# Norm weights spread by TensorE, places for all of o's split weights, v copied by ScalarE, and the query/key convolutions inside the heads' side chains

## The chip, the cores and the metric

The kernel runs on one core of a Trainium2 chip. The metric is the device time of one execution in microseconds (us). Engines are named as in the profile: PE is the matrix engine (PEld its weight loads), DVE the vector engine, ACT the scalar engine with the activation functions, POOL the general engine, SP the engine that issues the DMAs.

## The reference

One layer of a hybrid decoder trunk, T = 1024 tokens and D = 1024 channels, all in float32:

```
h = rms_norm(x, norm_pre_w)
proj = h @ w_in                       # columns for s5, pool, sconv, mlstm (qk, v, o, i, f), z paths, gates
qk = silu(causal_depthwise_conv(qk, conv_w))      # 4 taps, q and k, 4 heads of 128
y_d = mlstm(q, k, v, sigmoid(o), i, f)            # chunks of 64, exponential gates
y_a = s5_ssm(...); y_b = pool_mixer(...); y_c = short gated convolution
branches = y * silu(z)
merged = sum_b sigmoid(gate_b) * (branch_b @ w_branch[b])
out = x + rms_norm(merged @ w_out, norm_post_w)
```

## The kernel before

Each float32 matmul operand is split into a high and a low part (ACT copies the high part, DVE or POOL subtracts it from the operand for the low part), and a product takes three matmuls: high by high, high by low, low by high. One matmul of 128x512 is called a *mm* here.

The front of the program: `phase0` loads x in 8 tiles of 128 tokens. `norm(t)` squares a tile on ACT, works out the root on DVE with tiny operations, and multiplies by root and norm weights (`wpre`, the 4 KB row spread over 128 partitions by a 512 KB DMA) on DVE, at L332; `turn(t)` transposes the tile on PE (`tp`, L341) and splits it into `bh` (ACT, L344) and `bl` (DVE, L345). For the first two tiles the orders of SP, ACT, DVE and POOL are those of the program text; then a scheduler orders every engine from the text's priorities, and pools with a fixed count of places add waits. `load_vectors` fetches small vectors (`vrows`), `if_weights` the 8 columns of the mLSTM's input and forget gates (`ifraw`, 1,024 rows of 32 bytes) and splits them into two tiles `wif`. v's projection takes 24 mm for each of 8 tiles (L364), whose sum is copied from PSUM as `vst` and stored. `if_proj` takes 32 mm with `wif`; its sums `ifp` are copied by ACT to `ifsb` (L447), turned on PE (`iftp`, L455) and made into the gates by a chain of small DVE and ACT operations that ends in `lf` and a matmul `bps` (L480). o's projection has the same form as v's, with 8 weight tiles split into `o2h` (ACT) and `o2l` (POOL). `combos` forms sums of the operand's quarters (`t1f`, `t2f`, `t3f`, on DVE and POOL, L376, and split into `bht` and `blt`), with which the further products are made by Strassen's scheme, seven products of 12 mm for four quarters.

Then four heads: `qk_pair(h)` makes one such set of seven products (84 mm) for q and k into four tiles `xc`, and runs the 4-tap convolution on each: ACT scales the first tap into `cacc` (L561), DVE adds three taps (L563), ACT takes the sigmoid (L565), POOL multiplies (L566). `mlstm_head(h)` is a *side chain*: a generator that emits one step each time the main text ticks it, once after each product. Beside the chain, the main text emits the S5 inputs (heads 0 and 1) and gate products (heads 2 and 3). A product's two groups of 12 mm may share one PSUM bank, whose first contents are moved by an ACT copy `p<-p` (L213) before the second group may begin. Afterwards comes the S5 stage (`s5_gen`, a long DVE chain that first delivers `wr` to the PE transposes `wps`), beside more gate products, and then the gated paths, merges and the output.

The places for split weights, and the wait that the head's chain has before its first scores:

```
CFG = {"wr": 4, "w": 8, "ws": 3, "u": 3, "g": 12, "m": 4, "mm": 5, "sd": 3, "g2": 17}
def alloc(n):
    if len(self.wo) < 4:
        return self.wp.tile([P, HALF], F32R, tag="w", name=self.nm(n))
    return self.slot(n, dt=F32R)          # a place of "g"
...
prep(0)
for _ in range(ML_TICKS):                 # 3
    yield
scores(0)
```

Of the kernel before, what the change touches and what calls it, by code (L numbers as in the profile page):

```python
# [31 lines left out]
EARLY = ((0,), (1,), (2,), (3, 4))  # L32
ORDER = (3, 0, 1, 2)
PACE = 2
ML_TICKS = 3
DMA_SCRATCH = 1024
CFG = {"wr": 4, "w": 8, "ws": 3, "u": 3, "g": 12, "m": 4, "mm": 5, "sd": 3, "g2": 17}
MAGIC = 12582912.0
# [10 lines left out]
class Kern:  # L49
# [48 lines left out]
            return self.g2.tile(list(shape), dt, tag="g2", name=self.nm(name))  # L98
        return self.gp.tile(list(shape), dt, tag="g", name=self.nm(name))

    def stage(self, name, shape=(P, HALF)):
        return self.gp.tile(list(shape), F32, tag="m", name=self.nm(name))

    def u(self, name, shape=(P, HALF)):
        return self.wp.tile(list(shape), F32, tag="u", name=self.nm(name))
# [141 lines left out]
    def phase0(self):  # L247
        nc, io = self.nc, self.io
        x, wpre = io["x"], io["norm_pre_w"]
        names = ("11", "12", "21", "22")  # L250
        self.B = {n: (self.blk([P, 4, HALF], F32R, "bh" + n), self.blk([P, 4, HALF], F32R, "bl" + n)) for n in names}
        self.wv, self.wo = [], []
        wb = self.blk([P, D], F32, "wpre")
        self.warm_up()
        xs = {}

        def load(t, parts):
            xs[t] = self.blk([P, 2, D], F32, "x")
            n = D // parts
            for i in range(parts):  # L260
                nc.sync.dma_start(out=xs[t][:, 0, i * n:(i + 1) * n], in_=x[0, t * P:(t + 1) * P, i * n:(i + 1) * n])

        E = mybir.EngineType
        with self.tc.manual_schedule(engines={E.SP, E.Activation, E.DVE, E.Pool}):
            load(0, 2)
            nc.sync.dma_start(out=wb, in_=wpre.partition_broadcast(P))
            raw = [self.wp.tile([P, HALF], F32, tag="wr" if k < 4 else "ws", name=self.nm("raw")) if k < 7 else self.stage("raw")
                   for k in range(8)]
            hl = []
            for k in range(8):  # L270
                two = k < 6
                hl.append((self.slot("o2h", dt=F32R, two=two), self.slot("o2l", dt=F32R, two=two)))
            self.wv = hl

            def fetch(k):
                nc.sync.dma_start(out=raw[k], in_=io["w_in"][0, k * P:(k + 1) * P, C_V:C_V + HALF])

            def hi(k):
                nc.scalar.activation(out=hl[k][0], in_=raw[k], func=AF.Copy)

# [12 lines left out]
            lo(1, ve)  # L293
            self.turn(0, xs[0])
            hi(3)
            lo(2, po)
            lo(3, ve)
            self.norm(1, xs[1], wb)
            for k in range(4, 8):
                hi(k)  # L300
                lo(k, po if k % 2 == 0 else ve)
            self.turn(1, xs[1])
        for t in range(2, 8):
            load(t, 1)
            self.norm(t, xs[t], wb)
            self.turn(t, xs[t])
# [114 lines left out]

    def if_weights(self):
        nc = self.nc
        raw = self.u("ifraw", (P, 8, 8))
        nc.sync.dma_start(out=raw, in_=self.io["w_in"][0, :, C_IF:C_IF + 8].rearrange("(k p) c -> p k c", p=P))
        self.wif = []
        for kk in range(2):
            w = self.wp.tile([P, 4, P], F32R, tag="w", name=f"wif{kk}")
            r = raw[:, kk * 4:kk * 4 + 4, :]
            nc.gpsimd.memset(w.bitcast(F32), 0.0)  # L430
            nc.vector.tensor_copy(out=w[:, :, 0:8], in_=r)
            nc.vector.tensor_tensor(out=w[:, :, 8:16], in0=r, in1=w[:, :, 0:8].bitcast(F32), op=ALU.subtract)
            self.wif.append(w)

    def if_proj(self):
        nc = self.nc
        self.ifsb = []
        for hf in range(2):
            ps = self.bank("ifp")
            n = 0  # L440
            for i in range(2):
                for k in range(8):
                    nc.tensor.matmul(out=ps, lhsT=self.wif[k // 4][:, k % 4, :], rhs=self.B[f"{k // 4 + 1}{hf + 1}"][i][:, k % 4, :],
                                     start=(n == 0), stop=(n == 15))
                    n += 1
            sb = self.u("ifsb", (16, HALF))
            nc.scalar.activation(out=sb, in_=ps[0:16, :], func=AF.Copy)  # L447
            self.ifsb.append(sb)
# [93 lines left out]
    def qk_pair(self, h):  # L542

        nc = self.nc
        xc = {(i, hf): None for i in range(2) for hf in range(2)}

        def dest(i, hf):
            xc[i, hf] = self.slot("xc", (P, HALF + 3), two=True)
            return xc[i, hf][:, 3:HALF + 3], lambda t: t
        self.strassen(C_QK + h * P, C_QK + W + h * P, dest)  # L550
        out = []
        for i in range(2):
            ct = i * 4 + h
            w = lambda k: self.vec[:, k * 8 + ct:k * 8 + ct + 1]
            nc.gpsimd.memset(xc[i, 0][:, 0:3], 0.0)
            nc.vector.tensor_copy(out=xc[i, 1][:, 0:3], in_=xc[i, 0][:, HALF:HALF + 3])
            res = []
            for hf in range(2):
                x = xc[i, hf]
                acc = self.slot("cacc", two=True)  # L560
                nc.scalar.activation(out=acc, in_=x[:, 0:HALF], func=AF.Copy, scale=w(0))  # L561
                for k in range(1, 4):
                    nc.vector.scalar_tensor_tensor(out=acc, in0=x[:, k:k + HALF], scalar=w(k), in1=acc, op0=ALU.mult, op1=ALU.add)  # L563
                sg = x[:, 0:HALF]
                nc.scalar.activation(out=sg, in_=acc, func=AF.Sigmoid)  # L565
                nc.gpsimd.tensor_tensor(out=acc, in0=acc, in1=sg, op=ALU.mult)  # L566
                res.append(acc)
            out.append(res)
        return out

    def mlstm_head(self, h, qT, kT):

        nc = self.nc
        sc = float(P) ** -0.5
        cols = slice(h * P, (h + 1) * P)
        st = {}

        def prep(hf):
            hs_ = slice(hf * HALF, (hf + 1) * HALF)
# [88 lines left out]
            nc.sync.dma_start(out=self.yscr[3][cols, d["hs_"]], in_=y)  # L668

        prep(0)  # L670
        for _ in range(ML_TICKS):
            yield
        scores(0)
        prep(1)
        yield
        states(0)
        yield
        outputs(0, 0)
# [621 lines left out]
    def run(self):  # L1300
        nc, tc = self.nc, self.tc
        self.setup()
        with tc.tile_pool(name="g2a", bufs=CFG["g2"]) as self.g2:
            self.phase0()
            self.load_vectors()
            rc = self.const.tile([P, 16], F32, name="rcnt")
            rci = self.const.tile([P, 16], I32, name="rcnti")
            nc.gpsimd.iota(rci, pattern=[[1, 16]], base=1, channel_multiplier=0)
            nc.vector.tensor_copy(out=rc, in_=rci)
            nc.vector.reciprocal(out=rc, in_=rc)  # L1310
            self.rcnt = rc
            self.if_weights()
            for t in range(8):
                ps = self.proj_o2(self.wv, t)
                st = self.u("vst")
                nc.vector.tensor_copy(out=st, in_=ps)
                nc.sync.dma_start(out=self.vscr[t * P:(t + 1) * P, :], in_=st)
            self.if_proj()

# [15 lines left out]
            self.combos_last(full)
            between = (lambda: self.s5_u(0), lambda: self.s5_u(2), lambda: None, lambda: None)
            for h in range(4):
                qT, kT = self.qk_pair(h)
                self.sides.append(self.mlstm_head(h, qT, kT))
                between[h]()  # L1340
                for n in EARLY[h]:
                    self.keep_gates(*GATES[n])
            self.drain()
# [82 lines left out]
```

## Time and profile before

| | |
|---|---|
| device time, median of 3 runs | 1312.68 us (1310.72 to 1317.19) |
| profiled execution, device time | 1319.64 us |
| its span | 1317.9 us |
| PE busy in the span | 1250.6 us (95%) |
| DVE, POOL, ACT busy | 887.5, 714.5, 508.6 us |
| granted PE clock, mean | 0.972 of full speed |

The profile is one execution; every time below is on its clock, which starts with the span. It lies 7 us above the median of the runs. In a timeline row the two numbers are start and duration, and the brackets hold the idle time of the engine just before, with what ended it.

### The profile page before, as it was taken

Reading aid. Unit: us, or ns where it says so; the run is one execution under the profiler, and the core shown is the slowest. Engines: PE = TensorE matmul, PEld = TensorE weight load, DVE = VectorE, ACT = ScalarE, POOL = GpSimd, SP = SyncE. Lnnn points to the kernel's source line nnn. Section 1 sums busy time; section 2 is a strip of 40 time slices with the busy share of each in tenths; the row PEclk is TensorE's granted clock in tenths of the full one; section 3 lists DMA queues with packets and bytes.
Section 4 is the critical chain, followed back from the end, with each engine's and each line's share of the span. In section 5 each row is a group of like instructions: output and inputs, shape, how many; then the busy total and the mean of one; then the engine's idle time right before and its main releaser. Section 6 shows DMA issues by size and latency. Waiting matters only on the chain.

```text
span 1317.9 us, 17475 instructions
## 1 busy us (share of the span) xinstructions
PE 1250.6 (95%) x5790; PEld 1009.6 (77%) x5790; DVE 887.5 (67%) x1481; ACT 508.6 (39%) x930; POOL 714.5 (54%) x568
## 2 busy tenths in 40 slices
PE   7989999999989989999999989999999989979997
PEld 5867778787778757677778867888788868858886
DVE  7693886868774988689966776576856375443433
ACT  6223536365555433323344734233322232333221
POOL 4271675857555546455545454555575656678340
PEclk8989999999989989899999999999999999979999
DMA  7301333434435334443544666345554565597441
GB/s 237 109 25 64 98 111 114 113 112 108 124 102 140 93 84 112 105 116 93 142 114 137 167 193 217 98 154 155 182 171 150 161 191 155 185 370 248 126 154 48
DMA packets 211210, 183.76 MB, mean 139 GB/s; under 512 B 35916, under 2 KB 155296, under 8 KB 211120
## 3 DMA queue, kind: packets, MB, share of 16 engines
q1 hardware_dynamic: 211120, 182.65, 46.3%
q8 instruction: 46, 0.75, 0.2%
q14 instruction: 44, 0.36, 0.1%
HBM read 125.94 MB, written 54.56 MB: 137 GB/s over the span
## 4 chain that ended last, share of the span: by engine, by line
PE 58%; DVE 10%; DMA 6%; issue 3%; POOL 3%; ACT 1%; SPq 0%; DVEq 0%; POOLq 0%; ACTq 0%
PE p L155 35%; PE br L155 11%; PE out L155 7%; DMA raw<-in_w_in_dram 3%; DVE s L207 2%; POOL wlo L134 2%; DMA y<-yscr 1%; PE glu L155 1%; DMA raw<-in_w_branch_dram 1%; PE yps L1098 1%; PE yps L1097 1%; PE xps L1063 0%; PE yps L1100 0%; DVE Z L1080 0%; DMA m<-mscr 0%
## 5 line engine op out<-in xcount | busy, mean ns | idle before, releaser
L134 POOL TENSOR_TENSOR wlo<-raw,whi 128x512 fp32r<-128x512 f32 x166 | 234.1, 1412 | 223.2 <-ACT whi L130 146.2
L134 POOL TENSOR_TENSOR wlo<-s,whi 128x512 fp32r<-128x512 f32 x152 | 219.5, 1445 | 146.9 <-ACT whi L130 72.1
L155 PE MATMUL p<-bht,whi 128*128 128x512 f32 x608 | 170.3, 397 | 3.5 <-DVE u L201 1.6
L155 PE MATMUL p<-blt,whi 128*128 128x512 f32 x608 | 167.1, 394 | 0.0
L155 PE MATMUL p<-bht,wlo 128*128 128x512 f32 x608 | 166.2, 393 | 0.0
L130 ACT ACTIVATE whi<-raw 128x512 fp32r<-128x512 f32 x166 | 102.5, 618 | 156.7 <-PE p L155 94.2
L155 PE MATMUL p<-bh,whi 128*128 128x512 f32 x456 | 128.9, 403 | 17.0 <-ACT p L213 5.5
L130 ACT ACTIVATE whi<-s 128x512 fp32r<-128x512 f32 x152 | 95.0, 626 | 126.2 <-PE p L155 104.0
L207 DVE TENSOR_TENSOR s<-raw,raw 128x512 f32<-128x512 f32 x76 | 69.4, 913 | 99.2 <-DMA raw<-in_w_in_dram 84.2
L155 PEld LDWEIGHTS p<-bht,whi 128*128 128x128 f32 x608 | 113.2, 189 | 29.2 <-issue 4.4
L155 PEld LDWEIGHTS p<-blt,whi 128*128 128x128 f32 x608 | 114.5, 190 | 23.9 <-issue 0.2
L155 PEld LDWEIGHTS p<-bht,wlo 128*128 128x128 f32 x608 | 113.7, 189 | 23.6 <-issue 0.2
L155 PE MATMUL p<-bl,whi 128*128 128x512 f32 x456 | 128.3, 401 | 0.0
L155 PE MATMUL p<-bh,wlo 128*128 128x512 f32 x456 | 124.2, 393 | 0.5 <-POOL wlo L134 0.5
L155 PEld LDWEIGHTS p<-bh,whi 128*128 128x128 f32 x456 | 85.2, 191 | 38.3 <-ACT p L213 6.8
L155 PEld LDWEIGHTS p<-bl,whi 128*128 128x128 f32 x456 | 87.7, 194 | 18.7
L155 PEld LDWEIGHTS p<-bh,wlo 128*128 128x128 f32 x456 | 86.6, 191 | 19.7 <-POOL wlo L134 1.4
L155 PE MATMUL br<-yzh,whi 128*128 128x512 f32 x256 | 74.0, 405 | 12.0 <-ACT yzh L130 11.4
L155 PE MATMUL br<-yzl,whi 128*128 128x512 f32 x256 | 69.7, 392 | 0.0
L155 PE MATMUL br<-yzh,wlo 128*128 128x512 f32 x256 | 68.5, 389 | 0.0
L155 PEld LDWEIGHTS br<-yzh,whi 128*128 128x128 f32 x256 | 49.7, 195 | 24.6 <-ACT yzh L130 13.3
L1204 DVE TENSOR_TENSOR sg<-br,sg 128x512 f32<-128x512 f32 x64 | 43.6, 686 | 36.1 <-PE br L155 23.3
(433 smaller groups left out, 2222.3 us busy)
## 6 DMA issues: line engine op xcount, KB each, us to landing
raw<-in_w_in_dram SPq DMA_DIRECT2D x168, 256.0 KB
gscr<-sg SPq DMA_DIRECT2D x64, 256.0 KB
sg<-gscr SPq DMA_DIRECT2D x64, 256.0 KB
y<-yscr SPq DMA_DIRECT2D x48, 256.0 KB
mscr<-sg SPq DMA_DIRECT2D x48, 256.0 KB
m<-mscr SPq DMA_DIRECT2D x48, 256.0 KB
raw<-in_w_branch_dram SPq DMA_DIRECT2D x40, 256.0 KB
x<-in_x_dram SPq DMA_DIRECT2D x18, 256.0 KB
```

Source lines behind the costliest of these rows:

```text
L130: nc.scalar.activation(out=hi, in_=src, func=AF.Copy)
L134: eng.tensor_tensor(out=lo, in0=src, in1=hi.bitcast(F32), op=ALU.subtract)
L155: self.nc.tensor.matmul(out=out, lhsT=a(k), rhs=b(k), start=(n == 0 and not more), stop=(n == last), skip_group_check=more)
L207: tt(out=t, in0=a, in1=b, op=op)
L1097: nc.tensor.matmul(out=yps[gp][:, jj, :], lhsT=Tt[:, gl, :], rhs=V[:, gl, :], start=True, stop=False)
L1098: nc.tensor.matmul(out=yps[gp][:, jj, :], lhsT=car[q, jj, 0:8, :].rearrange("q d p -> q (d p)"), rhs=X[q, 0, jj, :], start=False, stop=False)
L1204: nc.vector.tensor_tensor(out=sg, in0=bps, in1=sg, op=ALU.mult)
```

## The change

It has four parts. The row of norm weights is loaded as 4 KB, before x, and spread by two matmuls of a column of ones with it, each 512 columns wide, whose results DVE copies into `wpre`. The gate columns go into one constant tile `wif` of 240 columns, of which overlapping slices of 128 columns are the weights; the split parts of v's last two weight tiles go to the places of "m", and one raw tile to a place of "u", so that the 8 places of "w" and the 12 of "g" hold nothing when o's weights come. v's copy out of PSUM goes from DVE to ACT. The convolution leaves `qk_pair` and becomes part of the head's side chain, with a yield after each DVE step of a pair of tiles; the chain has 14 steps where it had 11.

```diff
-ML_TICKS = 3
+            nc.sync.dma_start(out=wrow, in_=wpre)
             load(0, 2)
-            nc.sync.dma_start(out=wb, in_=wpre.partition_broadcast(P))
+            for i in range(2):
+                ps = self.bank("wps")
+                nc.tensor.matmul(out=ps, lhsT=ones, rhs=wrow[:, i * HALF:(i + 1) * HALF], start=True, stop=True)
+                nc.vector.tensor_copy(out=wb[:, i * HALF:(i + 1) * HALF], in_=ps)
...
-                two = k < 6
-                hl.append((self.slot("o2h", dt=F32R, two=two), self.slot("o2l", dt=F32R, two=two)))
+                alloc = (lambda n: self.slot(n, dt=F32R, two=True)) if k < 6 else (lambda n: self.stage(n, dt=F32R))
+                hl.append((alloc("o2h"), alloc("o2l")))
...
-        for kk in range(2):
-            w = self.wp.tile([P, 4, P], F32R, tag="w", name=f"wif{kk}")
...
+        self.wif = self.const.tile([P, 8 * 16 + 112], F32R, name="wif")
+        nc.gpsimd.memset(self.wif.bitcast(F32), 0.0)
+        w = self.wif[:, 0:P].rearrange("p (k c) -> p k c", c=16)
+        nc.vector.tensor_copy(out=w[:, :, 0:8], in_=raw)
+        nc.vector.tensor_tensor(out=w[:, :, 8:16], in0=raw, in1=w[:, :, 0:8].bitcast(F32), op=ALU.subtract)
...
+    def qk_conv(self, h, xc, out, i, hf):
+        acc = out[i][hf] = self.slot("cacc", two=True)
+        nc.scalar.activation(out=acc, in_=x[:, 0:HALF], func=AF.Copy, scale=w(0))
+        for k in range(1, 4):
+            nc.vector.scalar_tensor_tensor(out=acc, in0=x[:, k:k + HALF], scalar=w(k), in1=acc, op0=ALU.mult, op1=ALU.add)
+            yield
+        sg = x[:, 0:HALF]
+        nc.scalar.activation(out=sg, in_=acc, func=AF.Sigmoid)
+        nc.gpsimd.tensor_tensor(out=acc, in0=acc, in1=sg, op=ALU.mult)
...
+        def conv(hf):
+            pair = [self.qk_conv(h, xc, out, i, hf) for i in range(2)]
+            while pair:
+                pair = [g for g in pair if next(g, self) is not self]
+                if pair:
+                    yield
...
         prep(0)
-        for _ in range(ML_TICKS):
-            yield
+        yield from conv(0)
+        yield
         scores(0)
         prep(1)
-        yield
+        yield from conv(1)
         states(0)
...
-                nc.vector.tensor_copy(out=st, in_=ps)
+                nc.scalar.activation(out=st, in_=ps, func=AF.Copy)
...
-                qT, kT = self.qk_pair(h)
-                self.sides.append(self.mlstm_head(h, qT, kT))
+                xc = self.qk_pair(h)
+                self.sides.append(self.mlstm_head(h, xc))
```

The orders of the engines move at three places. First DVE at the start of the program; before, where `x_130` is the first tile of x and the L326 to L243 rows its root:

```order
L1310 RECIPROCAL rcnt_425<-rcnt_425 128x16
L326 TENSOR_TENSOR ssq_168<-ssq_169 128x1
L234 TENSOR_SCALAR rv_173<-ssq_168 128x1
L236 RECIPROCAL rr_174<-rt_175 128x1
L238 SCALAR_TENSOR_TENSOR rt_175<-rr_174,rv_173 128x1
L242 TENSOR_SCALAR rt_175<-rt_175 128x1
L243 TENSOR_TENSOR rr_174<-rr_174,rt_175 128x1
L332 SCALAR_TENSOR_TENSOR x_130<-x_130,rr_174,wpre_110 128x512 x2
```

And DVE at the same place with the change (`x_134` is the first tile of x, `wps` the spread norm weights in PSUM):

```order
L1321 RECIPROCAL rcnt_434<-rcnt_434 128x16
L436 CAST wif_441<-ifraw_439 128x8x8
L437 TENSOR_TENSOR wif_441<-ifraw_439,wif_441 128x8x8
L272 COPY wpre_110<-wps_137 128x512
L272 COPY wpre_110<-wps_140 128x512
L332 TENSOR_TENSOR ssq_177<-ssq2_178 128x1
L233 TENSOR_SCALAR rv_182<-ssq_177 128x1
L235 RECIPROCAL rr_183<-rt_184 128x1
L237 SCALAR_TENSOR_TENSOR rt_184<-rr_183,rv_182 128x1
L241 TENSOR_SCALAR rt_184<-rt_184 128x1
L242 TENSOR_TENSOR rr_183<-rr_183,rt_184 128x1
L338 SCALAR_TENSOR_TENSOR x_134<-x_134,rr_183,wpre_110 128x512 x2
```

The gate-column operations on `ifraw` stood behind the second tile's norm; they now stand ahead of the first norm, and so do two copies. On SP `ifraw` is now the twelfth DMA (behind the row, x, four raw tiles and four small vectors); it was the sixteenth.

The second place is ACT where v's projection ends and o's begins; before:

```order
L447 ACTIVATE ifsb_681<-ifp_664 16x512
L130 ACTIVATE bht_142_754<-t1f_794 128x512
L130 ACTIVATE o2h_722<-raw_720 128x512
L447 ACTIVATE ifsb_700<-ifp_683 16x512
L130 ACTIVATE bht_138_750<-t2f_799 128x512
```

With the change, the same stretch (`t2f_804` is here what `t2f_799` was, the third block's sum):

```order
L1327 ACTIVATE vst_638<-o_108_613 128x512
L129 ACTIVATE bht_142_757<-t3f_769 128x512
L129 ACTIVATE bht_144_759<-t1f_761 128x512
L129 ACTIVATE bht_144_759<-t1f_780 128x512
L129 ACTIVATE bht_140_755<-t2f_785 128x512
L1327 ACTIVATE vst_666<-o_110_641 128x512
L129 ACTIVATE bht_142_757<-t3f_788 128x512
L451 ACTIVATE ifsb_686<-ifp_669 16x512
L129 ACTIVATE bht_144_759<-t1f_799 128x512
L129 ACTIVATE bht_140_755<-t2f_804 128x512
L451 ACTIVATE ifsb_705<-ifp_688 16x512
```

The second `ifsb` now stands behind the split of the third block's t2, and v's copies stand between the splits, which wait for DVE's sums. On PE both halves of `iftp` now stand together, 24 mm (one o tile) behind the last mm of `if_proj`; 13 rows lay between them before. From the first `t1f` sum on, PE has 50 mm of v, the 32 of `if_proj` and these 24 before `iftp`.

The third place is PE in head 3, from the product's group that completes the last `xc` to the second group in the bank of the next product; before (`p_648` makes `xc`, and `p_732`'s first contents are what ACT's `p<-p` moves):

```order
L155 MATMUL p_648_3122<-bh_7_108,wlo_3167 128x512 x4
L155 MATMUL p_683_3282<-bht_138_750,wlo_3279 128x512 x4
...
L155 MATMUL p_705_3380<-bht_196_1181,wlo_3377 128x512 x4
L155 MATMUL p_732_3490<-bh_1_102,whi_3486 128x512 x4
L155 MATMUL p_732_3490<-bl_2_103,whi_3486 128x512 x4
L155 MATMUL p_732_3490<-bh_1_102,wlo_3487 128x512 x4
...
L155 MATMUL p_740_3520<-bht_140_752,wlo_3517 128x512 x4
L155 MATMUL p_732_3490<-bh_5_106,whi_3612 128x512 x4
```

With the change (`p_635` makes the last `xc`, and `p_715` is the bank in question):

```order
L154 MATMUL p_635_3073<-bh_7_108,wlo_3164 128x512 x4
L154 MATMUL p_666_3197<-bh_5_106,whi_3286 128x512 x3
...
L154 MATMUL p_704_3366<-bht_198_1186,wlo_3363 128x512 x4
L154 MATMUL p_715_3421<-bh_1_102,whi_3417 128x512 x4
L154 MATMUL p_715_3421<-bl_2_103,whi_3417 128x512 x4
L154 MATMUL p_715_3421<-bh_1_102,wlo_3418 128x512 x4
...
L154 MATMUL p_735_3497<-bht_140_755,wlo_3494 128x512 x4
L154 MATMUL p_715_3421<-bh_5_106,whi_3554 128x512
```

Between the first and the last of these rows lay 53 mm, and now 72: another product's 11 and `p_735`'s 12 come in, and 4 go. On ACT, the copy `p_715` now stands behind all four sigmoids of the head; before, it stood behind the table load and the first of them. DVE's twelve tap steps stand in one run at both, with two other sums among them. Further on, PE's order of the S5 stage begins 31 mm later in the program (the first `wps`) and ends 6 mm later (the last `yps`).

## Rows read from the trace of the kernel before

**Rows 1.** The page, part 1: busy time, share of the span, instructions.

```profile
PE 1250.6 (95%) x5790; PEld 1009.6 (77%) x5790; DVE 887.5 (67%) x1481; ACT 508.6 (39%) x930; POOL 714.5 (54%) x568
```

**Rows 2.** Stretches: length, busy times, granted PE clock, DMA share, GB/s.

```profile
0.00:10.00 10.00, 5.67 (x16) 2.25 (x17) 3.44 (x13) 3.85 (x9) 2.15 (x12) 0.96 0.77 247
0.00:134.00 134.00, 120.14 (x521) 92.47 (x522) 91.80 (x153) 51.83 (x97) 54.75 (x47) 0.94 0.33 108
370.00:380.00 10.00, 10.00 (x47) 8.37 (x46) 4.90 (x9) 4.53 (x8) 10.00 (x9) 0.78 0.21 77
480.00:690.00 210.00, 204.35 (x1104) 158.08 (x1100) 173.27 (x312) 68.93 (x132) 107.62 (x89) 0.98 0.43 112
```

**Rows 3.** Timeline of the first 14 us.

```profile
5.38 0.16 DVE L326 TENSOR_TENSOR ssq<-ssq 128x1 f32<-128x1 f32 x1 [3.28 <-ACT x L325]
...
8.68 1.41 DVE L332 SCALAR_TENSOR_TENSOR x<-x,rr,wpre 128x512 f32<-128x512 f32 x2 [1.88 <-DMA wpre<-in_norm_pre_w_dram]
9.24 1.30 ACT L279 ACTIVATE o2h<-raw 128x512 fp32r<-128x512 f32 x2 [3.28 <-DMA raw<-in_w_in_dram]
...
9.57 0.66 PE L341 MATMUL tp<-ident,x 128*128 128x128 f32 x2 [2.78 <-DVE x L332]
...
13.16 0.41 SPq L425 DMA_DIRECT2D ifraw<-in_w_in_dram  x1
```

**Rows 4.** DMA packets of the stretch 14.8 to 15.2 us.

```profile
DMA packets 279, 0.06 MB, mean 153 GB/s; under 512 B 253, under 2 KB 253, under 8 KB 279
```

**Rows 5.** The tiles vst and ost: count, min/median/max ns, first and last start.

```profile
L1316 DVE COPY vst<-o x8: 667/680/692, 23.6 to 79.0; 128x512 f32<-128x512 f32 x8
L1330 ACT ACTIVATE ost<-o x8: 591/598/603, 105.9 to 134.3; 128x512 f32<-128x512 f32 x8
```

**Rows 6.** Timeline from 60 to 112 us.

```profile
60.34 0.68 DVE L376 TENSOR_TENSOR t1f<-bh,bh 128x512 f32<-128x512 f32 x1
...
79.75 0.50 PE L364 MATMUL o<-o2h,bh 128*128 128x512 f32 x1 [2.06 <-DVE vst L1316]
...
81.97 0.60 PE L455 MATMUL iftp<-ident,ifsb 16*128 16x16 f32 x4 [1.72 <-ACT ifsb L447]
...
82.50 2.50 PE L364 MATMUL o<-o2h,bh 128*128 128x512 f32 x5
...
86.70 0.80 PE L364 MATMUL o<-o2h,bh 128*128 128x512 f32 x1 [1.70 <-ACT o2h L130]
...
88.74 1.76 DVE L376 TENSOR_TENSOR t2f<-t2f,bl 128x512 f32<-128x512 f32 x1
...
111.42 0.41 PE L480 MATMUL bps<-lf,tri 128*128 128x32 f32 x2 [1.11 <-DVE lf L477]
```

**Rows 7.** Timeline from 356 to 372 us, head 3.

```profile
356.34 1.16 PE L155 MATMUL p<-bht,whi 128*128 128x512 f32 x4 [0.77 <-DVE xc L194]
...
357.80 1.40 DVE L563 SCALAR_TENSOR_TENSOR cacc<-xc,vec,cacc 128x512 f32<-128x512 f32 x2
...
358.26 1.07 PE L155 MATMUL p<-bht,wlo 128*128 128x512 f32 x4
...
363.70 1.07 PE L155 MATMUL p<-bht,wlo 128*128 128x512 f32 x4
...
366.96 1.28 ACT L565 ACT_TABLE_LOAD   x1 [5.10 <-DVE cacc L563]
...
368.79 0.58 ACT L213 ACTIVATE p<-p 128x512 f32<-128x512 f32 x1
...
369.40 1.77 DVE L563 SCALAR_TENSOR_TENSOR cacc<-xc,vec,cacc 128x512 f32<-128x512 f32 x1
369.42 2.07 PE L155 MATMUL p<-bh,whi 128*128 128x512 f32 x4 [4.66 <-ACT p L213]
```

**Rows 8.** Waits of PE from 384 to 690 us: total, times, longest.

```profile
PE wps L1033 <- DVE wr L827: 5.9, 2, 5.7
```

More of the change, by code (lines that the diff above doesn't have):

```diff
@@ L99, in slot, with stage @@
         return self.gp.tile(list(shape), dt, tag="g", name=self.nm(name))
-    def stage(self, name, shape=(P, HALF)):
-        return self.gp.tile(list(shape), F32, tag="m", name=self.nm(name))
+    def stage(self, name, shape=(P, HALF), dt=F32):
+        return self.gp.tile(list(shape), dt, tag="m", name=self.nm(name))
     def u(self, name, shape=(P, HALF)):
@@ L254, in phase0 @@
         self.warm_up()
+        wrow = self.blk([1, D], F32, "wrow")
+        ones = self.const.tile([1, P], F32, name="ones")
+        nc.vector.memset(ones, 1.0)
         xs = {}
@@ L264, in phase0 @@
         with self.tc.manual_schedule(engines={E.SP, E.Activation, E.DVE, E.Pool}):
+            nc.sync.dma_start(out=wrow, in_=wpre)
             load(0, 2)
-            nc.sync.dma_start(out=wb, in_=wpre.partition_broadcast(P))
-            raw = [self.wp.tile([P, HALF], F32, tag="wr" if k < 4 else "ws", name=self.nm("raw")) if k < 7 else self.stage("raw")
+            for i in range(2):
+                ps = self.bank("wps")
+                nc.tensor.matmul(out=ps, lhsT=ones, rhs=wrow[:, i * HALF:(i + 1) * HALF], start=True, stop=True)
+                nc.vector.tensor_copy(out=wb[:, i * HALF:(i + 1) * HALF], in_=ps)
+            raw = [self.wp.tile([P, HALF], F32, tag="wr" if k < 4 else "ws", name=self.nm("raw")) if k < 7 else self.u("raw")
                    for k in range(8)]
@@ L423, in if_weights @@
         nc = self.nc
-        raw = self.u("ifraw", (P, 8, 8))
+        raw = self.const.tile([P, 8, 8], F32, name="ifraw")
         nc.sync.dma_start(out=raw, in_=self.io["w_in"][0, :, C_IF:C_IF + 8].rearrange("(k p) c -> p k c", p=P))
-        self.wif = []
-        for kk in range(2):
-            w = self.wp.tile([P, 4, P], F32R, tag="w", name=f"wif{kk}")
[L429 to L433, printed above, removed]
+        self.wif = self.const.tile([P, 8 * 16 + 112], F32R, name="wif")
[3 more added lines that the diff above has]
+        nc.vector.tensor_tensor(out=w[:, :, 8:16], in0=raw, in1=w[:, :, 0:8].bitcast(F32), op=ALU.subtract)
     def if_proj(self):
@@ L442, in if_proj @@
                 for k in range(8):
-                    nc.tensor.matmul(out=ps, lhsT=self.wif[k // 4][:, k % 4, :], rhs=self.B[f"{k // 4 + 1}{hf + 1}"][i][:, k % 4, :],
+                    nc.tensor.matmul(out=ps, lhsT=self.wif[:, k * 16:k * 16 + P], rhs=self.B[f"{k // 4 + 1}{hf + 1}"][i][:, k % 4, :],
                                      start=(n == 0), stop=(n == 15))
@@ L550, in qk_pair, with mlstm_head @@
         self.strassen(C_QK + h * P, C_QK + W + h * P, dest)
-        out = []
         for i in range(2):
-            ct = i * 4 + h
-            w = lambda k: self.vec[:, k * 8 + ct:k * 8 + ct + 1]
             nc.gpsimd.memset(xc[i, 0][:, 0:3], 0.0)
             nc.vector.tensor_copy(out=xc[i, 1][:, 0:3], in_=xc[i, 0][:, HALF:HALF + 3])
[L557 to L571, printed above, removed]
+        return xc
+    def qk_conv(self, h, xc, out, i, hf):
+        nc = self.nc
+        ct = i * 4 + h
+        w = lambda k: self.vec[:, k * 8 + ct:k * 8 + ct + 1]
+        x = xc[i, hf]
+        acc = out[i][hf] = self.slot("cacc", two=True)
[6 more added lines that the diff above has]
+        nc.gpsimd.tensor_tensor(out=acc, in0=acc, in1=sg, op=ALU.mult)
+    def mlstm_head(self, h, xc):
         nc = self.nc
@@ L576, in mlstm_head @@
         st = {}
+        qT, kT = out = {}, {}
+        def conv(hf):
[4 more added lines that the diff above has]
+                    yield
         def prep(hf):
```

## The prediction

> **What bounds the kernel now.** I read the busy times first: PE works 95% of the span and the next engine 67% [rows 1], so the change can only matter where PE waits or runs below its full clock. Then the stretches, to find where that is. From the start to 134 us, about where the first Strassen product begins, PE is idle for 13.9 us, far more than its share [rows 2]: the front half is not PE's. Then the timelines of the places that the order moves. At the start PE waits for the first tile's norm until 9.57 us, and that waits for the spread norm weights: the root is ready at 8.68 - 1.88 = 6.80 us, and 1.88 us of waiting for the DMA of `wpre` follow [rows 3]. Between v and o, PE stops for v's copy (2.06), for `ifsb` (1.72), for a split weight that had no place (1.70) and for `lf` (1.11), and works slowly between: five mm begun at 82.50 last 2.50 us [rows 6], where at full clock 24 mm take 363.70 - 358.26 = 5.44 us, 0.227 each [rows 7]. Last, head 3: 4.66 us of waiting for the copy `p<-p`, after which the granted clock of the next ten microseconds is 0.78 [rows 2, 7].
>
> **The start.** The 512 KB of `wpre` go; the two matmuls that spread the row stand where PE idles anyway, so they cost nothing (if PE did not idle there, two operations of the order of a microsecond each; no row shows one). But `ifraw`'s split now stands on DVE ahead of the first norm. When does `ifraw` land? SP's twelfth DMA waits for the semaphore of the fourth, so until the first raw tile has landed. That was at 9.24 us behind `wpre`; 512 KB at the 247 GB/s of this stretch are 2.1 us, so 7.1 now [rows 2, 3]. Before, from its issue at 13.16 its 32-byte packets ran until 15.2 us [rows 3, 4], 2.0 us; so it lands at 9.1. Then come the split (two operations; I take 0.4), two PSUM copies like v's at 0.68 [rows 5], and the root's chain, from 5.38 to 6.80, 1.4 us [rows 3]: the norm's product starts at 12.3 instead of 8.68, +3.6 us. Bounds: raw tiles not earlier at all gives 14.4, +5.7; a first raw tile two microseconds sooner still gives +1.6. What follows gives part of it back: v's raw tiles no longer queue behind 512 KB, and DVE, which the early norms need, loses the later gate split and v's copies of 0.68. I estimate 2.4 us of DVE work less by 30 us, and so +1.2 us there.
>
> **Between v and o.** v's eight copies cost ACT 0.6 each (as o's did) rather than DVE 0.68 [rows 5]; ACT is busy for only 39% [rows 1], so it has the room, but it takes its work in order, and between v's copies stand splits that wait for DVE's sums. The places settle the 1.70 and v's wait of 2.06 goes with the reshuffled order. In their stead: the second `ifsb` is now queued behind the split of the third t2 sum. Before, the first t1f sum started at 60.34 and the third t2 sum ended at 88.74 + 1.76 = 90.50 [rows 6], 30.2 us later, with three of v's copies among DVE's work; without them (2.0) 28.2. A split and `ifsb`, 0.6 each, make 29.4. PE has 50 + 32 + 24 = 106 mm from the same event to `iftp`, 24.1 us. So PE waits about 5 us (bounds: 0 if DVE is quicker by that; 8 if POOL slows its sums). After a wait of 4.66 us the clock took the next ten at 0.78 [rows 2, 7], 4.4 us of them at half, which loses 2.2; with the remainder before 370 us, 2.5. Then `lf`: its chain was 1.1 late before [rows 6], and with o's mm now behind rather than ahead of `iftp`, I estimate 2.2. Sum after: 5.0 + 2.5 + 2.2 = 9.7. Sum before: 2.06 + 1.72 + 1.70 + 1.11 = 6.6, and the half clock: 14 mm between 82.5 and 91 us, each 0.23 too long, 3.2; 9.8 in all. What the places and ACT give, the queue takes again. Front in all: +1.2 - 0.1, so about +1.
>
> **Heads.** In heads 0 to 2 the tap steps still stand ahead of the next product's sums on DVE, nearly as before, so I cost them at nothing; the cover is PE's mm between, and without it the price would be that of head 3. In head 3, PE waits for `p<-p`, which stands behind sigmoids, which wait for taps. Before, the twelve taps ran from 357.80 to 369.40 + 1.77 = 371.17 [rows 7], 13.4 us with three sums between. Now the copy stands behind all four sigmoids: the `xc` sum with its latency 0.8, one sum 1.0, taps and two sums 12.7, sigmoid and copy 1.2, make 15.7 us after the product that completes `xc`. PE has 72 mm in that time, 72 x 0.227 = 16.3 us. So the wait vanishes with 0.6 to spare: 4.66 + 0.77 of waiting and 2.5 of half clock, 7.9 at best. The margin is thin; if 2 to 3 us of wait remain with some of the slow clock, 2 to 4 are won. I take -6 (-8 to -2). The Trainium skill (TensorE: Matmul & The Clock Gate, Back-to-back issue gap) gives about 216 ns for a mm of 512 columns at full clock. By it the cover would be 15.5 us, and the copy 0.2 us late; this trace's mm take 0.227, so I keep the margin.
>
> **Behind the heads.** The chain's steps now come later in the program, so S5's first `wps` stands 31 mm later, and its last `yps` 6 mm later: 25 mm, 5.7 us, less cover for the S5 chain. Before it had 5.65 us of PE idle in 480 to 690 us [rows 2], so it was nearly always covered, with little to spare. The 5.7 us of waiting for the first `wr` [rows 8] should stay: the mm ahead of it fall by 8 (1.8 us), and DVE has three sums fewer ahead of it (about 2). I take +1.5 (0 to +6).
>
> **Sum:** +1 - 6 + 1.5 = -3.5 on the profiled execution's 1319.64, so 1316 there. The median of the runs shown lies 7 lower, and the same difference gives 1309.2 as the time to measure. About 0.5% (6.6 us) is what a measurement of this kernel can tell from no change.
>
> **Rivals.**
> - *The front wait does not come.* The DVE sums were stretched by POOL and by v's copies; if the third t2 sum is ready 5 us sooner, `iftp` finds `ifsb` there and neither its 5.0 nor the 2.5 are paid. For it: o's POOL splits now have places and can be over before the sums begin. Against it: DVE's and POOL's sums are the same in number, and 1.76 for one of them [rows 6] is their price side by side. It gives 1309.2 - 7.5 = 1301.7.
> - *Slower: taps at the slow rate in head 3.* A pair of taps took 1.40, the last alone 1.77 [rows 7]. If all twelve were as slow, 21.2 us instead of 11 to 12, the copy behind all four sigmoids would come 9 us late where it was 4.66 late, with half clock behind it: not -6 but about +5, and with +1 and +1.5 it gives 1312.7 + 7.5 = 1320. It decides from a mean tap of about 1.4. For it: the run of taps now has no other engine's step between; against it, the mean before was near 1.0. The Trainium skill (GPSIMD Engine Reference, Specifications) has a rule of this kind: the engine shares its SBUF interfaces with VectorE, in contention with DVE instructions that have two SBUF inputs, as taps and sums have; this trace has both rates, and no row here shows that POOL is the cause.
> - *S5 uncovered* with no gain in the front: the full 6 for 1.5 brings 1314, no change.
> - *Nothing moves:* head 3's wait only shifts to `kp` or to the next xc; then +2.5, 1315.
>
> **How the numbers follow.** My forecast 0.48 (its own range 1303 to 1313); the front wait absent 0.22; the slow taps 0.13; S5 uncovered or nothing moved 0.17. Faster than 1306.1: all but a little of the second, 0.20, and a quarter of the forecast, 0.12: 0.32. Slower than 1319.2: most of the slow taps, 0.10, and 0.03 where S5 loses its cover as well as the front: 0.13. The rest, 0.55, is within. The range from 1299 to 1319 takes in the front rival with its bounds and leaves out most of the slow one.
>
> **What would show it.** Right: the first `tp` near 13 us with DVE waiting for `ifraw`'s DMA; a PE wait of 4 to 6 us at `iftp` for `ifsb`, with a granted clock below 0.8 behind it; the first Strassen product within 3 us of 134; no wait over 1 us for `p<-p` in head 3; yps in place within 6 us. Wrong: the first Strassen product before 130 us (the front gave more than I allow); a long wait on `kp` or `p` in any head (the side chains' taps late); or S5's `wr`, U or Z waits on PE growing by more than 6 us.

## The result and the profile after

The changed kernel takes 1326.52 us (median of 4 runs, 1326.4 to 1327.36), the kernel before 1312.03 beside it: a ratio of 1.0099 (95% interval 1.0069 to 1.0128): 1.0% slower, and above the forecast's range. The profiled execution took 1326.4, close to its median, while before's lay 7 us above its own; so the gap between the two traces (6.8 us of span) is smaller than that of the medians, and the comparison goes by milestones inside the traces.

The stretches of the kernel after; the columns are those of [rows 2]:

```profile
0.00:144.60 144.60, 121.19 (x526) 94.00 (x527) 89.46 (x146) 56.01 (x105) 54.22 (x46) 0.93 0.29 97
90.00:100.00 10.00, 5.47 (x22) 4.12 (x22) 9.16 (x9) 2.37 (x4) 8.11 (x6) 0.69 0.01 2
380.00:390.00 10.00, 3.95 (x16) 3.46 (x16) 8.79 (x9) 4.65 (x9) 10.00 (x7) 0.70 0.09 19
```

The first Strassen product begins at 144.6 us, where it began at 134.0. PE was busy for about as long until then (121.2, against 120.1), but idle for 23.4 instead of 13.9 us [rows 2]: the front lost 10.6 us, and 9.5 of it is idling. What PE waited for, with total, times and longest wait, from 0 to 145, 300 to 410 and 384 to 690 us:

```profile
PE tp L347 <- DVE x L338: 10.1, 2, 6.9
PE tp L347 <- DVE bl L351: 2.5, 1, 2.5
...
PE iftp L459 <- ACT ifsb L451: 4.5, 1, 4.5
PE bps L484 <- DVE lf L481: 3.4, 1, 3.4
...
PE p L154 <- ACT p L212: 6.0, 1, 6.0
...
PE wps L1044 <- DVE wr L838: 5.0, 1, 5.0
```

The waits between v and o are there as forecast, with a granted clock of 0.69 in the ten microseconds where the first of them lies. Two are not as forecast: 10.1 us for the first norms, more than was allowed for, and 6.0 for `p<-p` in head 3, which should have gone.

**The start**, as the timeline of the kernel after shows it:

```profile
6.69 0.41 SPq L431 DMA_DIRECT2D ifraw<-in_w_in_dram  x1
...
8.67 0.33 SPq L263 DMA_DIRECT2D x<-in_x_dram  x1
...
9.29 0.20 DVE L436 CAST wif<-ifraw 128x64 fp32r<-128x64 f32 x1 [7.18 <-DMA ifraw<-in_w_in_dram]
...
9.66 1.28 DVE L272 COPY wpre<-wps 128x512 f32<-128x512 f32 x2
...
11.23 0.20 ACT L234 ACTIVATE rt<-rv 128x1 f32<-128x1 f32 x1 [6.02 <-DVE rv L233]
11.34 1.65 ACT L285 ACTIVATE o2h<-raw 128x512 fp32r<-128x512 f32 x3
...
12.03 2.51 POOL L288 TENSOR_TENSOR o2l<-raw,o2h 128x512 fp32r<-128x512 f32 x2 [9.99 <-ACT o2h L285]
12.11 1.24 DVE L242 TENSOR_TENSOR rr<-rr,rt 128x1 f32<-128x1 f32 x1
...
13.38 2.38 DVE L338 SCALAR_TENSOR_TENSOR x<-x,rr,wpre 128x512 f32<-128x512 f32 x2
...
15.24 1.94 PE L347 MATMUL tp<-ident,x 128*128 128x128 f32 x8 [6.89 <-DVE x L338]
...
18.23 1.05 ACT L334 ACTIVATE x<-x 128x1024 f32<-128x1024 f32 x1
...
22.54 3.40 DVE L338 SCALAR_TENSOR_TENSOR x<-x,rr,wpre 128x512 f32<-128x512 f32 x2
...
24.32 0.66 PE L347 MATMUL tp<-ident,x 128*128 128x128 f32 x4 [3.21 <-DVE x L338]
```

`ifraw`, SP's twelfth DMA now and its seventeenth before, lands at 9.3 us and holds up DVE. DVE's root therefore holds up ACT for 6.02 us, and the splits of v's raw tiles stand behind it on ACT. So POOL's `o2l` begins just when DVE makes the norm, and beside it an operation on one column takes 1.24 us (its neighbours 0.15 to 0.22) and the norm's pair 2.38 (before 1.41 [rows 3]). SP has seven small loads ahead of x's second tile and the next raw tiles; it issues them some 0.6 us apart, and that tile at 8.67. The DMA engines fall silent meanwhile; their GB/s in forty slices from 4 to 14 us:

```profile
GB/s 213 295 270 205 328 295 377 385 295 320 363 328 187 109 108 126 88 62 11 2 2 2 1 1 1 1 50 34 34 34 66 230 311 410 459 361 385 401 402 401
```

That is 1.99 MB in these 10 us; the kernel before moved 3.08 MB in them, of which at most 0.52 MB are the transfer that was saved. So other loads came later. But this silence cost nothing directly: from 9.5 to 32.7 us no engine waits for a DMA. ACT squares x's second tile at 18.23 without waiting for its load; it had waited 3.38 us until 16.37 for the first tile's transposes.

Further on, POOL splits o's weights in one run, beside the norms:

```profile
29.44 8.94 POOL L133 TENSOR_TENSOR o2l<-raw,o2h 128x512 fp32r<-128x512 f32 x6 [4.05 <-ACT o2h L129]
```

The norms' pairs of products at 28.83 and 33.76 us took 2.45 and 3.48 us, and those at 38.82 and 51.43, when POOL was done, 1.42 each. Before had slow pairs too (3.55, 2.38 and 2.41 us), and seven such splits in its first 60 us where now there are eight; what the places add is measured in e8 and e9 below.

**Head 3**, in the timeline of the kernel after:

```profile
362.60 1.07 PE L154 MATMUL p<-bh,wlo 128*128 128x512 f32 x4
...
363.98 0.18 DVE L235 RECIPROCAL rr<-rt 128x4 f32<-128x4 f32 x1 [1.35 <-ACT rt L234]
...
366.46 0.67 DVE L193 TENSOR_TENSOR xc<-p,u 128x512 f32<-128x512 f32 x1
...
369.02 0.69 DVE L206 TENSOR_TENSOR s<-raw,raw 128x512 f32<-128x512 f32 x1 [1.89 <-DMA raw<-in_w_in_dram]
...
369.63 1.78 DVE L568 SCALAR_TENSOR_TENSOR cacc<-xc,vec,cacc 128x512 f32<-128x512 f32 x1
...
371.93 9.80 DVE L568 SCALAR_TENSOR_TENSOR cacc<-xc,vec,cacc 128x512 f32<-128x512 f32 x10
...
379.15 1.07 PE L154 MATMUL p<-bht,wlo 128*128 128x512 f32 x4
...
383.33 1.75 DVE L568 SCALAR_TENSOR_TENSOR cacc<-xc,vec,cacc 128x512 f32<-128x512 f32 x1
...
385.10 0.63 ACT L571 ACTIVATE xc<-cacc 128x512 f32<-128x512 f32 x1 [2.13 <-DVE cacc L568]
385.64 0.58 ACT L212 ACTIVATE p<-p 128x512 f32<-128x512 f32 x1
...
386.27 0.80 PE L154 MATMUL p<-bh,whi 128*128 128x512 f32 x1 [6.05 <-ACT p L212]
```

The product that completes the last `xc` ends at 363.67, PE's cover at 379.15 + 1.07 = 380.22, and the copy at 386.22.

### The profile page after: what moved, and what is told of

Read it like the earlier page. It is cut to its first block, busy times and chain, and to the rows that moved or that the text cites. A ratio compares the mean times of both kernels' runs of the same rounds, so it can differ in the third digit from the quotient of the medians.

```text
span 1324.7 us, 17442 instructions
## 1 busy us (share of the span) xinstructions
PE 1249.9 (94%) x5794; PEld 1010.9 (76%) x5794; DVE 879.6 (66%) x1474; ACT 513.1 (39%) x938; POOL 709.0 (54%) x567
## 4 chain that ended last, share of the span: by engine, by line
PE 49%; DVE 10%; DMA 5%; issue 4%; POOL 2%; ACT 1%; SPq 0%; DVEq 0%; POOLq 0%; ACTq 0%
PE p L154 28%; PE br L154 10%; PE out L154 7%; DMA raw<-in_w_in_dram 2%; POOL wlo L133 1%; DVE s L206 1%; PE glu L154 1%; DMA raw<-in_w_branch_dram 1%; DMA y<-yscr 1%; PE yps L1108 1%; PE yps L1109 1%; DVE u L200 1%; DVE Z L1091 1%; PE yps L1111 0%; DMA T<-s5ks 0%
## 5 line engine op out<-in xcount | busy, mean ns | idle before, releaser
L133 POOL TENSOR_TENSOR wlo<-raw,whi 128x512 fp32r<-128x512 f32 x166 | 231.2, 1394 | 207.7 <-ACT whi L129 136.2
L133 POOL TENSOR_TENSOR wlo<-s,whi 128x512 fp32r<-128x512 f32 x152 | 215.9, 1421 | 183.8 <-ACT whi L129 92.0
L154 PE MATMUL p<-bht,whi 128*128 128x512 f32 x608 | 167.0, 393 | 0.0
L154 PE MATMUL p<-bh,whi 128*128 128x512 f32 x456 | 132.3, 406 | 16.3 <-ACT p L212 6.4
L206 DVE TENSOR_TENSOR s<-raw,raw 128x512 f32<-128x512 f32 x76 | 71.6, 942 | 107.4 <-DMA raw<-in_w_in_dram 97.4
L154 PE MATMUL br<-yzh,whi 128*128 128x512 f32 x256 | 73.8, 405 | 9.3 <-ACT yzh L129 9.3
```

Of the source, the lines that this page charges most:

```text
L133: eng.tensor_tensor(out=lo, in0=src, in1=hi.bitcast(F32), op=ALU.subtract)
L154: self.nc.tensor.matmul(out=out, lhsT=a(k), rhs=b(k), start=(n == 0 and not more), stop=(n == last), skip_group_check=more)
L206: tt(out=t, in0=a, in1=b, op=op)
```

## The experiments

Times are medians with the ratio to the kernel before, whose runs beside each had medians of 1312.0 to 1313.4. The other columns are starts (us) in one profiled execution of each: the first `tp`, the last mm of `if_proj`, the first Strassen product, the first `wps`; then the last `yps`.

| kernel | median | ratio (95%) | tp | if_proj | product | wps | yps |
|---|---|---|---|---|---|---|---|
| before | 1312.0 | 1 | 9.6 | 75.9 | 134.0 | 469.4 | 683.9 |
| after | 1326.5 | 1.0099 (1.0069 to 1.0128) | 15.2 | 85.4 | 144.6 | 488.7 | 695.0 |
| e1_no_row | 1321.4 | 1.0060 (1.0039 to 1.0080) | 8.7 | 79.6 | 138.7 | 481.0 | 688.7 |
| e2_only_row | 1320.1 | 1.0045 (1.0025 to 1.0065) | 15.0 | 83.4 | 140.5 | 475.5 | 683.5 |
| e3_no_conv | 1324.8 | 1.0080 (1.0053 to 1.0108) | 15.8 | 86.0 | 145.1 | 480.6 | 689.6 |
| e4_only_conv | 1316.6 | 1.0019 (0.9998 to 1.0040) | 9.2 | 75.5 | 133.6 | 476.7 | 683.8 |
| e5_late_small | 1327.1 | 1.0092 (1.0057 to 1.0127) | 13.6 | 84.2 | 143.6 | 486.6 | 695.2 |
| e6_split_late | 1329.1 | 1.0104 (1.0067 to 1.0142) | 13.1 | 86.9 | 144.4 | 488.3 | 697.4 |
| e7_only_copy | 1315.0 | 1.0012 (0.9989 to 1.0034) | 9.2 | 77.4 | 135.7 | 470.3 | 680.7 |
| e8_only_places | 1321.1 | 1.0051 (1.0033 to 1.0070) | 9.0 | 77.9 | 136.8 | 473.1 | 688.4 |
| e9_places_held | 1315.4 | 1.0031 (1.0013 to 1.0050) | 9.4 | 74.2 | 136.8 | 472.5 | 685.2 |
| e10_early_spread | 1325.4 | 1.0099 (1.0080 to 1.0117) | 8.9 | 82.7 | 142.1 | 484.6 | 692.3 |
| e12_before_early | 1316.9 | 1.0020 (1.0004 to 1.0035) | 8.1 | 79.7 | 138.1 | 473.1 | 686.1 |

**One part undone, or one part alone.** First the row (e1 is the changed kernel with this; e2 is the kernel before with the opposite edit):

```diff
-            nc.sync.dma_start(out=wrow, in_=wpre)
             load(0, 2)
-            for i in range(2):
...
+            nc.sync.dma_start(out=wb, in_=wpre.partition_broadcast(P))
```

> The changed kernel with the norm weights spread by the 512 KB transfer as before; the other three parts stay. Theory A (the row edit let the scheduler put the split of the gate columns and seven small transfers ahead of the first two tiles of x, and that is never given back): first tp near 9.6 us, v's projection over near 76 instead of 85 us, 9 to 10 us less than the changed kernel, so about 1317. Theory B (the free places are the cause: POOL's splits of o's weights run earlier and stretch DVE's norms): the late start remains in its greater part, over 1323.

> The kernel before with the row edit alone. Theory A: first tp near 15 us, and 8 to 10 us more than before, about 1321. Theory B: no more than the first delay of 3 to 4 us, about 1316 or less.

Undone, the first `tp` comes at 8.7 and the first product 5.9 us earlier; alone, it makes that product 6.5 later and the kernel 0.45% slower. The row is the largest part of the front's loss of 10.6 us. Undoing it wins back less than theory A had it (1321.4, not 1317, and the end of `if_proj` at 79.6, not 76): the other parts keep the rest. The stretch from the first `tp` to the end of `if_proj`, 66.4 us before and 70.2 after, is still 70.9 in e1. So between these two kernels the difference stands at the first tile (6.6 us) and is carried along (5.9 at the end of `if_proj` and at the first product).

Then the convolution (e3 is the changed kernel without its fourth part; e4 the kernel before with that part alone):

```diff
-        yield from conv(0)
-        yield
+        for _ in range(ML_TICKS):
+            yield
         scores(0)
```

> The changed kernel with the convolutions back ahead of the side chains. If moving them cost time in head 3 and behind it (theory A's second half), 1 to 4 us less than the changed kernel, near 1324; if the move gained what was forecast and only the start hid it (theory C), 5 us or more above the changed kernel, over 1331.

> The kernel before with the moved convolutions alone. Theory A's second half: a wait of 5 to 7 us for the copy behind the four sigmoids in head 3 again, 0 to 4 us more than before, 1312 to 1316. Theory C: that wait is under 1 us and the time 5 us or more below before, under 1307.

The first product of e4 stands at 133.6: the convolution costs the front nothing. In its heads PE waits for the copy as in the kernel after (waits from 300 to 410 us, e4):

```profile
PE p L154 <- ACT p L212: 6.1, 1, 6.1
```

and without the part (e3) its longest such wait is 4.6, as before [rows 7]:

```profile
PE p L155 <- ACT p L213: 5.0, 2, 4.6
```

Alone it comes to +0.19% with an interval that reaches just under nothing.

v's copy (e7), and the places for o's weights with the constant `wif` (e8), each alone on the kernel before:

```diff
-                nc.vector.tensor_copy(out=st, in_=ps)
+                nc.scalar.activation(out=st, in_=ps, func=AF.Copy)
```

> The kernel before with v's copies on ACT alone. Theory B (the places cost the other 5 us of the front): no change, first Strassen product 133 to 136 us, time within 3 us of before. Rival (ACT's order behind DVE's sums costs it): a wait of 4 us or more for the second ifsb, first Strassen product near 138.

```diff
+                alloc = (lambda n: self.slot(n, dt=F32R, two=True)) if k < 6 else (lambda n: self.stage(n, dt=F32R))
+                hl.append((alloc("o2h"), alloc("o2l")))
```

> The kernel before with the free places alone. Theory B: five or more of POOL's splits of o's weights in one run between 25 and 34 us, PE waiting 3 us more for DVE before 60 us, first Strassen product 136 to 139, 2 to 5 us more time. Rival: no change in the front or a gain of the 1.70 us that a split weight without a place cost.

The first product moves by +1.7 and +2.8. The places settle the wait for a split weight, and PE waits 8.3 us for `ifsb` in its stead (e8, from 60 to 140 us):

```profile
PE iftp L453 <- ACT ifsb L445: 8.3, 1, 8.3
```

As a time the places alone cost as much as the row, 0.51%, some 6.7 us; only 2.8 of that stands at the first product, and where the rest arises is open. As ratios the four parts alone add up to 0.45 + 0.19 + 0.12 + 0.51 = 1.27%, each known to about 0.2, and together they measured 0.99: no interplay is needed to explain the loss.

**The small loads late.** My theory was that the gate columns' load and split, put ahead of the first norm, were all of the row's cost:

```diff
             self.phase0()
-            self.load_vectors()
...
             self.turn(1, xs[1])
+            self.load_vectors()
+            self.if_weights()
```

> The changed kernel, with the loads and splits of the small vectors and gate columns written behind the second tile's turn in the ordered part, so that they stand behind x's second tile and v's weights on SP and behind both norms on DVE. Theory A: the whole cost of the row edit goes, the first Strassen product comes near 138 us as without the row edit (144.6 in the changed kernel), 5 to 7 us less time. Rival (the spread itself, two matmuls and two copies ahead of the first norm, is slow): first tp still over 11 us and less than 3 us gained.

In e6 the gate columns are loaded early and only their split comes late:

```diff
         self.warm_up()
+        self.if_weights()
...
             self.turn(1, xs[1])
+            self.if_split()
```

> The changed kernel with the split of the gate columns behind the first two norms on DVE, but all small transfers still ahead of x's second tile on SP. If DVE's wait for the gate columns is all of the row edit's cost, as e5: first Strassen product near 138. If the later transfers of x's second tile and v's last four weights matter by themselves, only the first 3 to 5 us of the start come back and the second tile's tp stays near 20 us or later: 140 to 143.

The theory fell. In e5 nothing of the gate columns is ahead of the norm, and the first `tp` comes at 13.6 instead of 15.2. e6 (13.1) is no better, and neither brings the first product forward by more than 1 us. Nor do the loads behind the small ones set the pace: e5 issues x's second tile at 5.16 us instead of 8.67, and the stretch from the first `tp` to the end of `if_proj` is no shorter, 70.6 us. The timeline of e5:

```profile
6.62 1.98 PE L271 MATMUL wps<-wrow,ones 1*128 1x512 f32 x4
7.78 0.69 DVE L272 COPY wpre<-wps 128x512 f32<-128x512 f32 x1 [5.66 <-PE wps L271]
8.64 0.69 DVE L272 COPY wpre<-wps 128x512 f32<-128x512 f32 x1 [0.17 <-PE wps L271]
...
9.62 0.20 ACT L234 ACTIVATE rt<-rv 128x1 f32<-128x1 f32 x1 [3.37 <-DVE rv L233]
...
10.42 2.51 POOL L288 TENSOR_TENSOR o2l<-raw,o2h 128x512 fp32r<-128x512 f32 x2 [8.61 <-ACT o2h L285]
10.49 1.24 DVE L242 TENSOR_TENSOR rr<-rr,rt 128x1 f32<-128x1 f32 x1
11.77 2.38 DVE L340 SCALAR_TENSOR_TENSOR x<-x,rr,wpre 128x512 f32<-128x512 f32 x2
```

The spread is not free. Its matmuls follow 14 warm-up matmuls and end at 8.6, and the root stands behind both copies on DVE. So ACT and POOL take v's splits late, and POOL's again lie beside the norm.

**The spread early.** Fewer warm-ups ahead of it, the copies on ACT behind the first root, and the small loads late: on the changed kernel (e10), and on the kernel before with the row alone (e12):

```diff
-WARM = 14
+WARM = 8
...
-                nc.vector.tensor_copy(out=wb[:, i * HALF:(i + 1) * HALF], in_=ps)
...
+            if spread:
+                nc.scalar.activation(out=wb[:, c], in_=spread[i], func=AF.Copy)
             nc.vector.scalar_tensor_tensor(out=hn[:, c], in0=xt[:, c], scalar=r, in1=wb[:, c], op0=ALU.mult, op1=ALU.mult)
```

> The changed kernel with the spread matmuls behind 8 instead of 14 warm-up matmuls, their copies on ACT behind the first root, and the small transfers late as in e5. Theory A in its mended form (the row edit's cost is that the first norm waits for a spread behind the warm-up, with its root's chain behind the copies, and then runs into POOL's first splits): first tp before 9.5 us, first Strassen product at 138 to 140 us (143.6 in e5), 4 to 6 us less than the changed kernel. Rival (the row edit costs through something later than the first norm): first tp early, but the first Strassen product still over 142 us.

> The kernel before with the norm weights spread as in e10 and nothing else of the change. Theory A mended: first tp 1 to 2 us before that of before, first Strassen product at 131 to 134 us, time within 0.4% of before on the faster side. Rival: still 3 us or more above before, as with the row edit alone.

The first `tp` now comes earlier than before (8.9 and 8.1), yet the first product stands at 142.1 and 138.1. So an early first tile alone does not win the time back: the stretch from it to the end of `if_proj` grows to 73.8 and 71.6 us. In e12's timeline the loss has moved to the third tile and v's remaining splits:

```profile
19.74 1.06 ACT L337 ACTIVATE x<-x 128x1024 f32<-128x1024 f32 x1 [5.55 <-DMA x<-in_x_dram]
20.80 0.61 ACT L286 ACTIVATE o2h<-raw 128x512 fp32r<-128x512 f32 x1
...
21.47 0.80 PE L375 MATMUL o<-o2h,bh 128*128 128x512 f32 x1 [3.52 <-ACT o2h L286]
```

ACT waits 5.55 us for x's third tile with a split of v's weights queued behind it, and PE waits 3.52 for that split. The tile itself is no later than before, where ACT squared it at 19.95; what is new is that ACT stands there early, with a split behind it. With the row alone made early, 0.25 of the 0.45% are won back, at intervals that overlap; it still does not beat the broadcast. Both kernels also have six warm-up matmuls fewer, and what that does was not measured apart.

**The places held.** Does the idling of e8 come from o's splits, which with free places run beside the norms? In e9 they wait for the sixth tile's root, through a factor of one made of it:

```diff
+            if t == 5:
+                nc.vector.tensor_scalar(out=self.one, in0=r, scalar1=0.0, scalar2=1.0, op0=ALU.mult, op1=ALU.add)
...
-        self.split(raw, hi, lo)
+        nc.scalar.activation(out=hi, in_=raw, func=AF.Copy, scale=self.one)
```

> The free places alone, as in e8, but the splits of o's weights wait for a column of ones that DVE makes behind the sixth tile's root, so that POOL cannot start them while the first norms run. Theory B: PE's waits for DVE before 60 us fall from 6.7 us of idle in e8 to 3 or 4, and the first Strassen product comes at 131 to 135 us instead of 136.8; 2 to 5 us less than e8. Rival (the cost is in what the places do after v, at iftp): idle before 60 us is the same as in e8 and the wait of 8.3 us for the second ifsb stays, no gain.

From 10 to 60 us PE idled 6.7 us in e8 and 1.9 in e9, so the splits did cost the norms, and the stretch from the first `tp` to the end of `if_proj` fell from 68.9 to 64.9 us. But the product stands at 136.8 in both. The waits of e9 from 60 to 140 us:

```profile
PE bps L483 <- DVE lf L480: 6.8, 1, 6.8
PE iftp L458 <- ACT ifsb L450: 3.8, 2, 3.1
```

The idling has only moved behind v, which neither theory had. e9 is faster than e8 by about 0.2%, at intervals that overlap, and its first product doesn't explain that; it stays open.

**The rate beside POOL**, in a program of these operations alone, without the layer:

```diff
+            for k in range(50):
+                nc.gpsimd.tensor_tensor(out=pa, in0=a, in1=b2, op=ALU.subtract)
+            for k in range(12):
+                nc.vector.scalar_tensor_tensor(out=o1, in0=a, scalar=s1[:, 0:1], in1=b2, op0=ALU.mult, op1=ALU.add)
```

> No trunk at all: only twelve taps, twelve PSUM copies, twelve differences of PSUM and SBUF, and twelve operations of one column on DVE, first with POOL idle and then beside 50 of POOL's 128x512 subtractions; the output is zeros. Theory B: taps 0.7 us alone and 1.4 to 1.8 beside POOL, PSUM copies 0.7 in both, one-column operations 0.16 alone and now and then over 1 us beside POOL. Rival (the slow taps come from elsewhere, as the scratch of a busy DMA or a late operand): under 0.8 us in both.

The groups by line, with busy time and mean ns; lines up to 1322 ran with POOL quiet, those from 1328 on beside L1325:

```profile
L1325 POOL TENSOR_TENSOR pa<-ta,tb 128x512 f32<-128x512 f32 x50 | 67.1, 1341 | 3.8
L1328 DVE SCALAR_TENSOR_TENSOR tap<-ta,tiny,tb 128x512 f32<-128x512 f32 x12 | 19.6, 1634 | 0.4
L1316 DVE SCALAR_TENSOR_TENSOR tap<-ta,tiny,tb 128x512 f32<-128x512 f32 x12 | 9.0, 752 | 2.9 <-DMA tb<-in_x_dram 2.5
...
L1320 DVE TENSOR_TENSOR sub<-pss,tb 128x512 f32<-128x512 f32 x12 | 8.3, 690 | 0.4
L1332 DVE TENSOR_TENSOR sub<-pss,tb 128x512 f32<-128x512 f32 x12 | 8.3, 690 | 0.4
...
L1334 DVE TENSOR_TENSOR tinyb<-tiny 128x1 f32<-128x1 f32 x12 | 6.7, 559 | 0.4
L1322 DVE TENSOR_TENSOR tinyb<-tiny 128x1 f32<-128x1 f32 x12 | 1.9, 158 | 0.4
```

A tap takes 0.75 us with POOL quiet and 1.63 beside it; with one operand in PSUM (`pss`) DVE takes 0.69 at both. Beside POOL the operations on one column took 1.11 us at the longest and 0.18 in the median. So POOL's subtractions are enough to slow operations with two SBUF inputs, as taps, sums and norms are, to rates near those of the kernel.

## Why the prediction was wrong

**The start: the step that failed.** The forecast was +3.6 us at the first `tp` and +1.2 by 30 us. It measured +5.7 at the first `tp` and +9.5 at the end of `if_proj`. The landing of `ifraw` (9.3, forecast 9.1), its split (0.4) and the two copies (1.3) were as costed. The root was costed at its length of before, 1.4, and took 2.5, and the product 1.0 more, because ACT, held up by the same delay, released POOL's splits onto them. And "gives part of it back" had the wrong sign: instead of 2.4 us less by 30 us, 3.8 more came between the first `tp` and the end of `if_proj` (70.2 us, before 66.4). I counted DVE work that goes, and put POOL's splits of o's weights, which lie beside the norms, at nothing. The trace has six of them in one run, with norms at 2.45 and 3.48 us instead of 1.42; e8 has 2.5 us more in this stretch with the places alone, and e9, which holds the splits back, 4.0 less than e8. Since the places add one split to seven, it must be where they fall beside the norms rather than their number; that is argued, and no run shows it apart. v's copy alone adds 1.8 there (e7); why is open. The row alone adds 2.0 (e2), but in the changed kernel undoing it does not shorten the stretch (e1, 70.9). The later loads of x and v's weights are not what does it, since no engine waits for them and e5, which issues x's second tile early, keeps the stretch (70.6). "Costs nothing" for the spread was wrong too: without `ifraw` in front of it, in e5, the spread and its copies start the root 3.9 us later than before (9.24, before 5.38). Of the first tile's 5.7 us the POOL overlap carries 1.1 in the root and 1.0 in the product by the trace; no run undid it there by itself.

**Between v and o: right in its rows.** The wait for `ifsb` was forecast at 5.0 and is 4.5, that for `lf` 2.2 and is 3.4, with the clock lower behind. From the end of `if_proj` to the first product it took 59.1 us, before 58.1: about +1, forecast -0.1. The rival in which this wait is absent fell.

**Head 3: the second step that failed.** The copy was to be ready 15.7 us after its product, with 16.3 of cover. The cover was 380.22 - 363.67 = 16.55, as costed; the copy took 22.55. Three terms were too small. The `xc` sum ended 3.46 us after the product instead of 0.8, since two sums and head 2's root stood ahead of it on DVE, the root waiting 1.35 for ACT. The one sum ahead of the taps took 2.5 instead of 1.0, of which 1.89 is waiting for a raw tile's DMA. The taps with two sums took 385.08 - 369.63 = 15.45 instead of 12.7, the first and last tap and a sum at 1.75 to 1.78 beside POOL. That is 2.7 + 1.5 + 2.7, less 0.1 in sigmoid and copy: 6.8 late, less the margin, 6.0 of wait. So the slower rival's place was right, but not its condition: the mean tap was (1.78 + 9.80 + 1.75) / 12 = 1.11 us, under the 1.4 from which it was to decide. Taps and sums together account for 2.7 of the 6.8, and two queues ahead of the taps, which I had not walked through, are the rest. The Trainium skill (GPSIMD Engine Reference, Specifications) says that POOL shares its SBUF interfaces with VectorE and contends with instructions of two SBUF inputs. e11 agrees: 0.75 against 1.63 us, and no change with a PSUM input.

**Behind the heads.** The wait for the first `wr` stayed (5.0, forecast 5.7). From the first product to the first `wps` the runs with the convolution in the chain took 342 to 344 us, those without 335 to 336; those 7 us are the 31 mm that the order puts ahead of the first `wps` (7.0 at 0.227), and no loss. From there to the last `yps` the order has 25 mm, 5.7 us, less. The runs with the convolution in the chain took 206 to 209 us there, those without 208 to 215 (before 214.5, in an execution 7 us above its median), some 4 less in the mean. So most of what was moved comes back, and head 3's gain is what is missing. The convolution alone ends at +2.5 us (-0.3 to +5.3), where -6 and +1.5 were forecast.

## What to carry to other kernels

A byte saved at the start is worth only what the first link of the chain gains: here 1.88 us of waiting for the spread weights went, and a load that lands at 9.3 us came ahead of the same norm. An idle DMA engine is no cost in itself; look for the engine that waits for the late load before blaming it. When an operation is put ahead of the first link of a chain, walk every in-order engine that waits for that link (here ACT, with the next weights' splits behind the root); what it releases late may run beside the very work that was delayed. The same holds for work that free places let start early: ask what it will run beside. A margin below a microsecond must be costed with the queue ahead of the first step and with the rate beside the other engine, not with a mean of before.

## What the runs showed of the hardware

Two things I had not expected. Beside POOL even DVE operations on a single column are stretched: from 0.16 to 0.56 us in the mean in e11, where the median is 0.18 and the longest 1.11, so some are held up and most are not. In the root at the start one took 1.24 us, so a chain of tiny operations is not immune. POOL loses as well: its subtraction had a median of 1.26 us in e11 and took up to 1.59, beside the taps. And the spread of one row by two matmuls of 512 columns took 1.98 us on PE, in four records: near a microsecond for each matmul, over four times the 0.227 of a mm.
